# A rank-16 adapter matmul: semaphores set by hand, and the scheduler's context closed behind the first loads

## The chip, the core and the metric

The kernel runs on one core of a Trainium2 chip. The metric is the device time of one execution in microseconds. The kernel before takes 165.16 us, the median of three runs (165.13 to 165.30).

Five engines run their own instruction streams: PE (TensorE: weight loads and matmuls), DVE (VectorE), ACT (ScalarE), POOL (GpSimd) and SP (SyncE, which here only issues DMAs). They meet through semaphores: an instruction may wait until a semaphore has reached a value, and may raise or lower one when it is done. A DMA raises its semaphore by 16 when it has landed, one for each of the 16 DMA engines that share the transfer.

## The reference

```
x_flat = x.reshape(-1, 256)                 # x: 16 x 2048 x 256, so 32768 rows
y = x_flat @ W                              # W: 256 x 256
lora_out = (x_flat @ lora_A) * lora_E       # lora_A: 256 x 16, lora_E: 16
y = y + scale * (lora_out @ lora_B)         # lora_B: 16 x 256, scale 1.0
```

All arrays are float32. The input x and the output have 33.55 MB each.

## The kernel before

The adapter is folded into the weights once: weff = W + lora_A diag(lora_E) lora_B, in bfloat16. PE transposes the two 128-row chunks of lora_A (L92), DVE scales the result by lora_E (ate, L94), PE multiplies it with lora_B (ps_aeb, L104), and DVE adds W (weff, L106). lora_B is first cast to bfloat16 (L89). The identity for the transposes is made on POOL (two instructions in masks.py).

The rows of x are cut into nine blocks of 16, 32 (seven times) and 16 rows for each of 128 partitions: 2 MB or 4 MB. Six buffers ("slots") in SBUF hold a block each. The result is written over the block's input in its slot and stored from there. Loads and stores are all issued by SP, in an order written out by hand: W (L74), loads 0 to 5 (L67), then for each block its store (L71), and behind store 2 the loads 6, 7 and 8, each of which needs the slot of store 0, 1 or 2 and so waits for that store's landing. ACT issues the loads of lora_A, lora_B and lora_E (L76, L78, L80).

A block is worked off in groups of two rows for each partition, 128 groups in all. For a group PE transposes four 128x128 pieces into psum_xt (L114, three buffers), DVE casts them to bfloat16 into xt (L120, four buffers), PE multiplies them with weff into psum_y (L132, three buffers), and ACT copies the result into the slot (L140). PE transposes group n + 1 ahead of the matmuls of group n. The store of a block waits for its last copy.

All of this lies in a tile scheduler's context. The order on each engine is the order of the text (manual_schedule), and the scheduler sets the semaphores: which instruction waits for what, and who raises what. When the context is left (L175) it has each engine drained, lets all engines meet, has POOL clear the semaphores, and lets them meet again. L161 makes the program object, whose start also has all engines meet once.

Of the kernel before, what the change touches and what calls it, by code (L numbers as in the profile page):

```python
# [1 line left out]

# [5 lines left out]

PLAN = [16] + [32] * 7 + [16]

ROWS, SLOTS = 32, 6

LEAD = 6
AFTER = {2: [6, 7, 8]}
CG = 2


@with_exitstack  # L20
def kernel(
    ctx: ExitStack,
    tc: tile.TileContext,
    x: bass.AP,
    W: bass.AP,
    lora_A: bass.AP,
    lora_B: bass.AP,
    lora_E: bass.AP,
    scale: bass.AP,
    out: bass.AP,  # L30
):
    nc = tc.nc
    P = 128
    FP32 = mybir.dt.float32
    BF16 = mybir.dt.bfloat16

    x_flat = x.flatten_outer_dims()
    out_flat = out.flatten_outer_dims()
    N, K = x_flat.shape
    M = out_flat.shape[1]  # L40
    R = lora_B.shape[0]
    KC = K // P
    assert K == M and sum(PLAN) * P == N

    const = ctx.enter_context(tc.tile_pool(name="const", bufs=1))
    slots = ctx.enter_context(tc.tile_pool(name="slots", bufs=SLOTS))
    xTpool = ctx.enter_context(tc.tile_pool(name="xTpool", bufs=4))
    ps_setup = ctx.enter_context(tc.tile_pool(name="ps_setup", bufs=1, space=bass.MemoryType.PSUM))
    ps_xT = ctx.enter_context(tc.tile_pool(name="ps_xT", bufs=3, space=bass.MemoryType.PSUM))
    ps_y = ctx.enter_context(tc.tile_pool(name="ps_y", bufs=3, space=bass.MemoryType.PSUM))  # L50


    ctx.enter_context(tc.manual_schedule())

    starts = [sum(PLAN[:i]) * P for i in range(len(PLAN))]

    def rows_of(flat, i):
        b, r0 = PLAN[i], starts[i]
        return flat[r0:r0 + b * P, :].rearrange("(p b) k -> p b k", b=b)

    held = []

    def load(i):
        t = slots.tile([P, ROWS, K], FP32, name="xy")
        nc.sync.dma_start(out=t[:, :PLAN[i], :], in_=rows_of(x_flat, i))  # L67
        held.append(t)

    def store(i):  # L70
        nc.sync.dma_start(out=rows_of(out_flat, i), in_=held[i][:, :PLAN[i], :])  # L71

    w_sb = const.tile([P, KC, M], FP32)
    nc.sync.dma_start(out=w_sb, in_=W.rearrange("(c p) m -> p c m", p=P))  # L74
    a_sb = const.tile([P, KC, R], FP32)
    nc.scalar.dma_start(out=a_sb, in_=lora_A.rearrange("(c p) r -> p c r", p=P))  # L76
    b_sb = const.tile([R, M], FP32)
    nc.scalar.dma_start(out=b_sb, in_=lora_B)  # L78
    e_sb = const.tile([R, 1], FP32)
    nc.scalar.dma_start(out=e_sb, in_=lora_E[:, None])  # L80

    for i in range(LEAD):
        load(i)

    ident = const.tile([P, P], FP32)
    make_identity(nc, ident)

    b_bf = const.tile([R, M], BF16)
    nc.vector.tensor_copy(out=b_bf, in_=b_sb)  # L89
    ps_at = ps_setup.tile([R, KC, P], FP32, name="ps_at")  # L90
    for c in range(KC):
        nc.tensor.transpose(ps_at[:, c, :], a_sb[:, c, :], ident)  # L92
    ate = const.tile([R, KC, P], BF16)
    nc.vector.tensor_scalar(  # L94
        out=ate,
        in0=ps_at,
        scalar1=e_sb,
        scalar2=float(scale),
        op0=mybir.AluOpType.mult,
        op1=mybir.AluOpType.mult,  # L100
    )
    ps_aeb = ps_setup.tile([P, KC, M], FP32, name="ps_aeb")
    for c in range(KC):
        nc.tensor.matmul(ps_aeb[:, c, :], ate[:, c, :], b_bf, start=True, stop=True)  # L104
    weff = const.tile([P, KC, M], BF16)
    nc.vector.tensor_add(out=weff, in0=w_sb, in1=ps_aeb)  # L106

    groups = [(i, g) for i, b in enumerate(PLAN) for g in range(b // CG)]

    def transposed(i, g):  # L110
        psum_xt = ps_xT.tile([P, CG, KC, P], FP32, name="psum_xt")
        for j in range(CG):
            for c in range(KC):
                nc.tensor.transpose(  # L114
                    psum_xt[:, j, c, :],
                    held[i][:, g * CG + j, c * P:(c + 1) * P],
                    ident,
                )
        xt = xTpool.tile([P, CG, KC, P], BF16, name="xt")
        nc.vector.tensor_copy(out=xt, in_=psum_xt)  # L120
        return xt


    ready = transposed(*groups[0])
    for n, (i, g) in enumerate(groups):
        xt = ready
        if n + 1 < len(groups):
            ready = transposed(*groups[n + 1])
        psum_y = ps_y.tile([P, CG, M], FP32, name="psum_y")
        for j in range(CG):  # L130
            for c in range(KC):
                nc.tensor.matmul(  # L132
                    psum_y[:, j, :],
                    xt[:, j, c, :],
                    weff[:, c, :],
                    start=(c == 0),
                    stop=(c == KC - 1),
                )

        nc.scalar.copy(out=held[i][:, g * CG:(g + 1) * CG, :], in_=psum_y)  # L140
        if (g + 1) * CG == PLAN[i]:
            store(i)
            for later in AFTER.get(i, []):
                load(later)


# [1 line left out]
_INS = ['x', 'W', 'lora_A', 'lora_B', 'lora_E', 'scale']  # L148
_OUTS = [((16, 2048, 256), 'float32')]

_NUMBERS = {'scale': 1.0}


# [26 lines left out]
```

## Time and profile before

| what | us |
|---|---|
| timed runs, median of three | 165.16 |
| span of the profiled execution, first to last instruction | 163.0 |
| what lies around the span (165.16 - 163.0) | 2.16 |
| PE busy in the span | 120.8 |
| DVE, ACT busy | 90.0, 76.3 |
| queue q1 (SP's loads and stores), share of 16 DMA engines | 96.7% |
| bytes moved, mean rate | 67.56 MB, 414 GB/s |

The profiled execution is one execution, taken by the hardware profiler; its own time is its span, and the time around it is known only against the timed runs. Busy shares are averages over the whole span; the page's table of 40 slices (4.1 us each) shows where they lie. The chain of waits follows the last instruction back to what released it. "SPq" is the queue of SP, in which it issues DMAs and waits. A DMA's issue (about 0.45 us on SP or ACT) is not its transfer; the time from issue to landing stands apart.

### The profile page before, as it was taken

The numbers are of one execution on the slowest core, as the hardware profiler recorded it, in microseconds if no ns is written. First come the engines' busy times: TensorE is split into PE (matmuls) and PEld (weight loads), VectorE is DVE, ScalarE is ACT, GpSimd is POOL, SyncE is SP. The second block draws the span as 40 slices with busy tenths as digits, with TensorE's granted clock in tenths as the row PEclk, the third lists the DMA queues.
The fourth block names the chain that finished last, engine by engine and source line by source line (L and its number), as shares of the span: only waits on it lengthen the run. The fifth ranks groups of instructions, "written<-read, shape, count | busy, mean of one in ns | idle before, by whom it ended". The sixth has DMA issues, their size and how long they took to land.

```text
span 163.0 us, 2547 instructions
## 1 busy us (share of the span) xinstructions
PE 120.8 (74%) x1028; PEld 100.9 (62%) x1028; DVE 90.0 (55%) x131; ACT 76.3 (47%) x129; POOL 0.7 (0%) x6
## 2 busy tenths in 40 slices
PE   0189799999999999999999799999999910000000
PEld 0068588888888888888888588888888800000000
DVE  0156477777777777777777667777777700000000
ACT  0036465666666665666666546665666620000000
POOL 1000000000000000000000000000000000000000
PEclk9999999999999999999999999999999995555555
DMA  5999999998998999999999999999999999999992
GB/s 151 428 474 434 394 491 398 410 491 382 420 474 386 392 410 466 418 438 418 450 430 418 442 434 402 432 450 418 422 434 442 422 442 426 442 418 434 434 394 113
DMA packets 3211, 67.56 MB, mean 414 GB/s; under 512 B 624, under 2 KB 896, under 8 KB 896
## 3 DMA queue, kind: packets, MB, share of 16 engines
q1 hardware_dynamic: 2864, 67.37, 96.7%
q8 instruction: 8, 0.13, 0.3%
q10 hardware_dynamic: 336, 0.03, 0.2%
q14 instruction: 3, 0.02, 0.0%
HBM read 33.85 MB, written 33.55 MB: 414 GB/s over the span
## 4 chain that ended last, share of the span: by engine, by line
DMA 55%; PE 23%; ACT 1%; SPq 1%; DVE 0%; issue 0%
DMA xy<-in_x_dram 28%; DMA out_dram<-xy 27%; PE psum_y L132 12%; PE psum_xt L114 11%; ACT xy L140 1%; DVE xt L120 0%; SPq L67 0%; SPq L74 0%
## 5 line engine op out<-in xcount | busy, mean ns | idle before, releaser
L120 DVE CAST xt<-psum_xt 128x512 bf16<-128x512 f32 x128 | 88.6, 692 | 32.5 <-PE psum_xt L114 32.5
L140 ACT COPY xy<-psum_y 128x512 f32<-128x512 f32 x128 | 75.0, 586 | 46.5 <-PE psum_y L132 46.5
L114 PE MATMUL psum_xt<-ident,xy 128*128 128x128 f32 x512 | 77.8, 276 | 2.6 <-DMA xy<-in_x_dram 2.6
L132 PE MATMUL psum_y<-weff,xt 128*128 128x256 bf16 x512 | 78.0, 275 | 0.3 <-DVE xt L120 0.3
L114 PEld LDWEIGHTS psum_xt<-ident,xy 128*128 128x128 f32 x512 | 60.8, 142 | 5.0 <-issue 2.9
L132 PEld LDWEIGHTS <-xt 128*128 128x128 bf16 x512 | 40.0, 98 | 17.0 <-DVE xt L120 0.9
L140 ACT ACT_TABLE_LOAD x1 | 1.3, 1283 | 9.3 <-DMA xy<-in_x_dram 9.3
L92 PE MATMUL ps_at<-ident,a_sb 128*16 128x128 f32 x2 | 0.6, 394 | 4.1 <-DMA a_sb<-in_lora_A_dram 4.1
L89 DVE CAST b_bf<-b_sb 16x256 bf16<-16x256 f32 x1 | 0.3, 281 | 5.8 <-DMA b_sb<-in_lora_B_dram 5.8
L104 PE MATMUL ps_aeb<-b_bf,ate 16*128 16x256 bf16 x2 | 0.6, 402 | 3.8 <-DVE ate L94 3.8
L104 PEld LDWEIGHTS <-ate 16*128 16x128 bf16 x2 | 0.1, 104 | 4.2 <-DVE ate L94 4.2
L92 PEld LDWEIGHTS ps_at<-ident,a_sb 128*16 128x16 f32 x2 | 0.1, 87 | 4.0 <-issue 4.0
L94 DVE TENSOR_SCALAR ate<-ps_at,e_sb 16x256 bf16<-16x256 f32 x1 | 0.5, 471 | 1.8 <-DMA e_sb<-in_lora_E_dram 1.8
L106 DVE TENSOR_TENSOR weff<-w_sb,ps_aeb 128x512 bf16<-128x512 f32 x1 | 0.7, 689 | 0.7 <-PE ps_aeb L104 0.7
masks.py:199 POOL TENSOR_SCALAR_AFFINE_SELECT ident<-ident 128x128 f32<-128x128 f32 x1 | 0.3, 292 | 0.1
masks.py:197 POOL MEMSET ident<- 128x128 f32 x1 | 0.2, 204 | 0.3 <-POOLq L161 0.3
L161 POOL MEMSET const-bfloat16-1.0<- 128x1 bf16 x1 | 0.1, 101 | 0.0
L161 POOL MEMSET const-uint8-127<- 128x1 uint8 x1 | 0.1, 101 | 0.0
L161 POOL MEMSET const-float32-0.0<- 128x1 f32 x1 | 0.1, 98 | 0.2 <-issue 0.2
L161 POOL MEMSET const-float32-1.0<- 128x1 f32 x1 | 0.1, 98 | 0.0
## 6 DMA issues: line engine op xcount, KB each, us to landing
xy<-in_x_dram SPq DMA_DIRECT2D x7, 4096.0 KB, 29.0
out_dram<-xy SPq DMA_DIRECT2D x7, 4096.0 KB, 37.4
xy<-in_x_dram SPq DMA_DIRECT2D x2, 2048.0 KB, 16.1
out_dram<-xy SPq DMA_DIRECT2D x2, 2048.0 KB, 36.9
w_sb<-in_W_dram SPq DMA_DIRECT2D x1, 256.0 KB, 3.0
a_sb<-in_lora_A_dram ACTq DMA_DIRECT2D x1, 16.0 KB, 3.2
b_sb<-in_lora_B_dram ACTq DMA_DIRECT2D x1, 16.0 KB, 4.5
e_sb<-in_lora_E_dram ACTq DMA_DIRECT2D x1, 0.1 KB, 6.0
```

The source lines that it names most:

```text
L89: nc.vector.tensor_copy(out=b_bf, in_=b_sb)
L92: nc.tensor.transpose(ps_at[:, c, :], a_sb[:, c, :], ident)
L94: nc.vector.tensor_scalar(out=ate, in0=ps_at, scalar1=e_sb, scalar2=float(scale), op0=mybir.AluOpType.mult, op1=mybir.AluOpType.mult,)
L104: nc.tensor.matmul(ps_aeb[:, c, :], ate[:, c, :], b_bf, start=True, stop=True)
L106: nc.vector.tensor_add(out=weff, in0=w_sb, in1=ps_aeb)
L114: nc.tensor.transpose(psum_xt[:, j, c, :], held[i][:, g * CG + j, c * P:(c + 1) * P], ident,)
L120: nc.vector.tensor_copy(out=xt, in_=psum_xt)
L132: nc.tensor.matmul(psum_y[:, j, :], xt[:, j, c, :], weff[:, c, :], start=(c == 0), stop=(c == KC - 1),)
L140: nc.scalar.copy(out=held[i][:, g * CG:(g + 1) * CG, :], in_=psum_y)
L161: nc = _bacc.Bacc("TRN2", target_bir_lowering=False, num_devices=1)
```

## The change

The context is closed inside the kernel function, and everything behind it is written without the scheduler.

- Buffers in SBUF and PSUM are taken from the program object directly, in the same number and size.
- Every semaphore is the kernel's own (class Count): one for each small input, for each load and for each store, and six for the steps of the engines.
- W's load and loads 0 to 5 are issued by SP in a block that is marked as critical, the three small loads by ACT in a second such block. Then the context is closed and compiled, so that what it does on leaving (drain, meeting, clearing, meeting) stands there.
- All that follows is the same work in the same order on each engine, with waits written out: two ahead of a group's matmuls (cast done, psum_y free), two ahead of its cast (transposes done, xt free), one ahead of its copy, one ahead of a store, one ahead of loads 6 to 8. PE waits for a load at a block's first group.
- At the end each engine waits for the final values of some semaphores and subtracts them, so that they are zero again: twelve on PE, five on DVE, one on ACT, ten on SP, the last of these for the last store.

The core of the diff (declarations of sizes and the unchanged launch left out):

```diff
+class Count:
+    def __init__(self, nc, name):
+        self.sem = nc.alloc_semaphore(name)
+        self.total = 0
+
+    def by(self, ins, n=1):
+        self.total += n
+        ins.then_inc(self.sem, n)
+        return self.total
...
-    ctx.enter_context(tc.manual_schedule())
...
     def load(i):
-        t = slots.tile([P, ROWS, K], FP32, name="xy")
-        nc.sync.dma_start(out=t[:, :PLAN[i], :], in_=rows_of(x_flat, i))
-        held.append(t)
+        s_ld[i].by(nc.sync.dma_start(out=slot(i), in_=rows_of(x_flat, i)), 16)
 
     def store(i):
-        nc.sync.dma_start(out=rows_of(out_flat, i), in_=held[i][:, :PLAN[i], :])
+        s_st[i].by(nc.sync.dma_start(out=rows_of(out_flat, i), in_=slot(i)), 16)
+
+    def spent(engine, count):
+        engine.wait_ge(count.sem, count.total).then_inc(count.sem, -count.total)
...
+    with tc.tile_critical(no_gpsimd_drain=True):
+        s_w.by(nc.sync.dma_start(out=w_sb, in_=W.rearrange("(c p) m -> p c m", p=P)), 16)
+        for i in range(LEAD):
+            load(i)
+    with tc.tile_critical(no_gpsimd_drain=True):
+        s_a.by(nc.scalar.dma_start(out=a_sb, in_=lora_A.rearrange("(c p) r -> p c r", p=P)), 16)
+        s_b.by(nc.scalar.dma_start(out=b_sb, in_=lora_B), 16)
+        s_e.by(nc.scalar.dma_start(out=e_sb, in_=lora_E[:, None]), 16)
+    tc.close()
+    tc.compile()
+
+    s_id.by(nc.gpsimd.memset(ident, 0.0))
+    nc.gpsimd.wait_ge(s_id.sem, 1)
+    s_id.by(nc.gpsimd.affine_select(
+        out=ident, in_=ident, compare_op=mybir.AluOpType.not_equal, fill=1.0, base=0,
+        pattern=[[-1, P]], channel_multiplier=1))
...
+    nc.vector.wait_ge(s_b.sem, 16)
+    s_v.by(nc.vector.tensor_copy(out=b_bf, in_=b_sb))
+    nc.tensor.wait_ge(s_a.sem, 16)
+    nc.tensor.wait_ge(s_id.sem, 2)
     for c in range(KC):
-        nc.tensor.transpose(ps_at[:, c, :], a_sb[:, c, :], ident)
+        at_done = nc.tensor.transpose(ps_at[:, c, :], a_sb[:, c, :], ident)
+    s_set.by(at_done)
+    nc.vector.wait_ge(s_e.sem, 16)
+    nc.vector.wait_ge(s_set.sem, 1)
...
-    def transposed(i, g):
-        psum_xt = ps_xT.tile([P, CG, KC, P], FP32, name="psum_xt")
+    def transposed(n):
+        i, g = groups[n]
+        if g == 0:
+            nc.tensor.wait_ge(s_ld[i].sem, 16)
         for j in range(CG):
             for c in range(KC):
...
+        s_t.by(done)
+        nc.vector.wait_ge(s_t.sem, n + 1)
+        if n >= 4:
+            nc.vector.wait_ge(s_m.sem, n - 3)
+        s_v.by(nc.vector.tensor_copy(out=xt[n % 4], in_=ps_xt[n % 3]))
...
+        nc.tensor.wait_ge(s_v.sem, ready0 + n + 1)
+        if n >= 3:
+            nc.tensor.wait_ge(s_y.sem, n - 2)
         for j in range(CG):
             for c in range(KC):
...
+        s_m.by(done)
+        nc.scalar.wait_ge(s_m.sem, n + 1)
+        s_y.by(nc.scalar.copy(out=slot(i)[:, g * CG:(g + 1) * CG, :], in_=ps_y[n % 3]))
         if (g + 1) * CG == PLAN[i]:
+            nc.sync.wait_ge(s_y.sem, n + 1)
             store(i)
             for later in AFTER.get(i, []):
+                nc.sync.wait_ge(s_st[later - SLOTS].sem, 16)
                 load(later)
+
+    for count in [s_a, s_id, s_v] + s_ld:
+        spent(nc.tensor, count)
+    for count in [s_b, s_e, s_w, s_set, s_t]:
+        spent(nc.vector, count)
+    spent(nc.scalar, s_m)
+    for count in [s_y] + s_st:
+        spent(nc.sync, count)
```

## The prediction

> **What bounds the kernel now.** I read the page's slices and queues first, then the chain, then SP's waits, then the timeline of the first 12 us, and last the rows of line 175.
>
> ```profile
> PE   0189799999999999999999799999999910000000
> ...
> DMA  5999999998998999999999999999999999999992
> ...
> q1 hardware_dynamic: 2864, 67.37, 96.7%
> ...
> DMA 55%; PE 23%; ACT 1%; SPq 1%; DVE 0%; issue 0%
> ```
>
> The DMA engines are full from the second slice to the last but one. Queue q1 (SP's loads and stores) fills 96.7% of 16 engines. PE ends in slice 33 of 40. So the span is: the time to the first packet, 67.37 MB at the rate of the engines, and what follows the last packet. Compute matters only if a store is issued so late that the queue runs empty.
>
> ```profile
> SPq L71 <- ACT xy L140: 85.7, 8, 14.3
> SPq L67 <- DMA out_dram<-xy: 32.7, 3, 14.1
> SPq L175 <- DMA out_dram<-xy: 29.5, 3, 15.1
> ```
>
> SP waits for compute before eight stores, and after the last one only for landings: compute is ahead of the queue. How far, the single records say. Stores 2, 7 and 8 are issued at 50.10, 124.78 and 132.12. The last packets of the transfers ahead of them (stores 1, 6 and 7) end at 73.9, 147.0 and 156.7. The first q1 packet (2.04) comes 1.3 us after its issue (0.74). So store 7 may be 147.0 - 1.3 - 124.8 = 20.9 us later before the slowest DMA engine is empty, store 2 22.5 us, store 8 23.3 us. Store 7 has the least cover.
>
> ```profile
> 0.73 0.50 ACTq L76 DMA_DIRECT2D a_sb<-in_lora_A_dram  x1
> 0.74 0.44 SPq L74 DMA_DIRECT2D w_sb<-in_W_dram  x1
> 1.23 3.53 SPq L67 DMA_DIRECT2D xy<-in_x_dram  x6
> 1.25 0.49 ACTq L78 DMA_DIRECT2D b_sb<-in_lora_B_dram  x1
> 1.77 0.44 ACTq L80 DMA_DIRECT2D e_sb<-in_lora_E_dram  x1
> ...
> 7.87 0.47 DVE L94 TENSOR_SCALAR ate<-ps_at,e_sb 16x256 bf16<-16x256 f32 x1 [1.83 <-DMA e_sb<-in_lora_E_dram]
> ...
> 11.16 1.03 PE L132 MATMUL psum_y<-weff,xt 128*128 128x256 bf16 x4
> ```
>
> All inputs are issued by 4.8 us, ACT's three beside SP's. The first real matmul (11.16) hangs on lora_E, although that is 64 bytes: it lands 6.0 us after its issue, behind A and B in q10.
>
> ```profile
> L175 POOLq EVENT_SEMAPHORE  x4: 17/17/17, 162.3 to 162.9; - x4
> L175 SPq DRAIN  x2: 7/7/7, 162.3 to 162.6; - x2
> ...
> L175 POOLq EVENT_SEMAPHORE_RANGE_CLEAR  x1: 96/96/96, 162.6 to 162.6; - x1
> ```
>
> That is line 175 after 162.3: two rounds of all engines with a semaphore clear between, until 163.0. The last q1 packet ends at 161.57, and SP's wait for it passes at 162.06.
>
> **The change part by part.** The profiled execution has a span of 163.0; the median of the timed runs is 165.16, so 2.16 us lie around the span, which I leave as they are.
>
> *Closing barriers gone from the end.* From SP's pass (162.06) to the end are 0.94 us: two more waits 0.06 apart, drains, two rounds. What comes instead are SP's ten waits that subtract; nine pass while earlier stores land, the tenth takes 0.03 to 0.06. Gain 0.88 to 0.91, on the path: -0.9.
>
> *Barriers at the front.* SP reaches them after its seven issues: 0.74 + 7 x 0.49 = 4.2. Two rounds took 0.64 at the end (162.31 to 162.95), so the other engines are free at about 4.9 (7 if ACT's block comes after). Cover: load 0 lands at 9.2 and lora_E at 7.8 or later. The identity's two POOL instructions (0.20 and 0.29) then end by 5.7, A's transposes (0.58) by 6.3: nothing. Entry into the first marked block: at least one semaphore step, 0.04 by the first barrier's rows (POOL 0.611, SP 0.653), at most a whole barrier (0.67, the span's first). I take 0.1, nearest to a step.
>
> *SP's load 4 no longer waits for lora_A's landing* (3.12 to 3.94): nothing, five transfers are queued ahead.
>
> *ACT's three loads in a second marked block.* The diff does not say whether block two may start before block one is over. Both ends: side by side, ACT issues at 0.73 as now; one after the other, ACT waits until SP has issued seven transfers, 4.2, plus a drain and two or three semaphore steps, 4.45. I take the later: the scheduler treats a marked block as one unit, ended by a drain of its engines, and keeps such units in order. Then what do A, B and E cost behind the bulk? Lower bound: the rows of now, 3.2, 4.5 and 6.0 us from issue to landing, so E at 5.5 + 6.0 = 11.5, 4 later than now. Upper bound, by the packet records: on one DMA engine A's 64-byte pieces start 49 ns apart as long as W's 1 KB pieces (46 ns) lie between, and 7 ns apart once W is through: one piece of each queue in turn. A has 256 pieces, 16 for each engine, and a completion. In the new order a turn is a piece of x: 0.61 us (16 KB, load 0) until 8.5, then 1.21 (32 KB). First piece 4.45 + 1.8 (A's 0.73 to 2.51) = 6.2; four turns to 8.5; thirteen more x 1.21 = 15.7: 24.2. B and E follow: now 3.5 us from A's end to E's, at 0.61 a turn 5.5 turns, then 6.7 us: 30.9, visible 0.4 later at 31.3 instead of 7.8. I take this end, since it is the same queue in the same trace.
>
> The Trainium skill ("DMA: Bandwidth & Descriptors", section on queues, rings and completion order) says an engine takes its queue rows in turn but drains a whole packet of some 9 to 17 descriptors each time. By that A would need one or two turns, and E would land near 12. The 49 ns do not agree with it.
>
> So the first matmul moves by 23.5 us. Two waits of compute for loads that are then long there fall away: 1.2 ahead of block 1 (PE's longest wait for a load) and 1.3 ahead of block 6 (store 5 at 95.45 against 50.10 + 3 x 14.67 = 94.11). Store 7 is 23.5 - 2.5 = 21.0 late, against a cover of 20.9: used up, 0.1 over. Store 2 is 22.3 late, against 22.5.
>
> *ACT's table load* (1.28 from 9.28, now while ACT waits) may come behind the first hand-written wait. Three psum_y buffers, 2.75 of PE's work, cover it.
>
> *Waits written by hand.* Each of 128 groups has two waits before its matmuls and two before its cast. Now the cast itself waits for PE, and weight load and matmul each carry one wait. By hand, the instruction behind can take one, and the other may stand ahead of it. A wait that stands ahead costs 0.075 before the instruction starts (ate's: 7.795, then 7.870; PE's: 3.953, then 4.029). PE and DVE wait for each other: from a group's transposes (41.09) over its cast (41.72) to its matmuls (42.47) are 1.38, PE has 1.31 of work meanwhile (three fours of 0.44), and two groups take 1.83 (casts at 39.89 and 41.72). A delay d in that loop costs d/2 a group. So 0 (both waits carried as now) to 0.075 a group (one ahead on each engine). I take the middle, 0.0375; there is no nearer row. To store 7 are 120 groups: 4.5 us (0 to 9). Alone it is hidden by the 20.9; behind the late weights it is not.
>
> A page has a price for this: "VectorE: DVE Perf Modes" in the Trainium skill, in its section on the drain that can't be avoided, found that a semaphore after each copy costs nothing extra. By that the sum would lose its 4.5; the 0.075 of the two rows speaks against.
>
> Sum for the likeliest case: 165.16 - 0.9 + 0.1 + 0.1 + 4.5 = **169.0 us**. In span, 166.8.
>
> **The rivals.**
> 1. *ACT's block runs beside SP's.* A, B and E are issued at 0.73 as now, E lands at 7.8, the waits cost at most 9 of 20.9: all hidden. 165.16 - 0.9 + 0.1 = 164.4: faster. For it: different engines, nothing shared in the trace's first microseconds. Against: the order of marked blocks.
> 2. *Late weights, free waits.* Blocks in order, but PE and DVE carry their waits as now. Store 7 is 0.1 over its cover, within the error of the 31.3: 164.4 to 165.0. It decides at a shift of 20.9 at store 7.
> 3. *A's pieces go through in one turn.* E near 12, shift of store 7 about 4 + 9 at most: hidden, 164.4. The Trainium skill's rule on packets above is this one; the 49 ns are against it.
> 4. *The first load is later.* If the entry into a block costs a whole barrier, 0.67, first packet at 2.7 and the gain is nearly gone: 165.16 - 0.9 + 0.7 = 165.0, no change.
>
> **How the numbers follow.** A measurement of this kernel tells some 0.2% from no change (164.83 to 165.49). Forecast case 0.56, of which 0.02 within 0.2%; rival 1 0.22; rival 2 0.11, of which 0.02 within; rival 3 0.05; rival 4 0.06, of which 0.04 within, 0.01 on each side. Faster 0.22 + 0.09 + 0.05 + 0.01 = 0.37; same 0.08; slower 0.54 + 0.01 = 0.55. The likeliest case alone goes from 165.7 (waits at 0.01 a group) to 173.5 (waits at 0.075: 9.0 in place of 4.5). Since faster cases hold more than 2 in 10, the range begins at theirs, 164.2.
>
> **What would show it.** Right: ACT's issue of lora_A at 4 to 5 us, ate at about 31, first matmul of line 132's successor near 34.5, casts 0.95 or more apart, store 7 issued after 146, and a hole in the DMA row at 75 to 80 or 147 to 152. Nothing of barriers after the last landing, and the span ending within 0.1 us of SP's last wait. Wrong: ACT's issues before 2 us, or ate before 15: then DMA stays full and the time is 164.4. A first q1 packet later than 2.5 would be rival 4. A compute rate of 0.917 a group with late weights is rival 2.

## The result and the profile after

The changed kernel takes **167.38 us** (median of four runs, 166.94 to 167.82), the kernel before 165.16 (median of four as well). The ratio is 1.0136, with a 95% interval of 1.0122 to 1.0150: slower. The profiled execution is the longest of the four, 167.82, with a span of 166.5 and 1.32 around it.

Rows of the page of the kernel after: busy tenths in 40 slices of 4.16 us, bytes moved in each, the chain that ended last, and the landing times of two of ACT's loads (the last number of the last two lines, us from issue to landing):

```profile
PE   0000001199999999999999999999999999999000
...
DMA  5999999999999999959899989999999999999994
GB/s 161 409 485 394 466 418 414 457 394 480 401 421 457 346 449 447 419 228 394 374 378 425 453 386 496 374 362 457 425 392 464 401 449 421 441 429 449 417 390 209
...
PE 72%; DMA 16%; DVE 1%; ACTq 1%; ACT 0%; issue 0%
...
a_sb<-in_lora_A_dram ACTq DMA_DIRECT2D x1, 16.0 KB, 23.5
...
e_sb<-in_lora_E_dram ACTq DMA_DIRECT2D x1, 0.1 KB, 26.3
```

PE starts its main work in the ninth slice instead of the third. The DMA row has one hole, in the 18th slice (70.8 to 74.9 us), where the rate falls to 228 GB/s. The chain that ended last was mostly DMA and is now 72% PE: it runs from lora_E's landing through PE to the stores. A chain of this kind says which work was late, not that PE is too slow: PE's busy time has hardly changed (121.5 us against 120.8).

The start of the span and the issue of store 2, from the timeline of the kernel after (start, length, engine, line, operation; in brackets the idle time ahead of it and what ended it):

```profile
0.94 0.44 SPq L84 DMA_DIRECT2D w_sb<-in_W_dram  x1
1.43 2.99 SPq L74 DMA_DIRECT2D xy<-in_x_dram  x6
5.03 0.43 ACTq L88 DMA_DIRECT2D a_sb<-in_lora_A_dram  x1
5.49 0.49 ACTq L89 DMA_DIRECT2D b_sb<-in_lora_B_dram  x1
6.00 0.44 ACTq L90 DMA_DIRECT2D e_sb<-in_lora_E_dram  x1
7.41 0.20 POOL L94 MEMSET ident<- 128x128 f32 x1 [6.97 <-POOLq L92]
...
32.31 0.47 DVE L110 TENSOR_SCALAR ate<-ps_at,e_sb 16x256 bf16<-16x256 f32 x1 [2.17 <-DMA e_sb<-in_lora_E_dram]
...
35.27 1.03 PE L148 MATMUL psum_y<-weff,xt 128*128 128x256 bf16 x4
...
73.97 0.33 SPq L77 DMA_DIRECT2D out_dram<-xy  x1
```

ACT's first issue stands at 5.03, 0.6 behind the end of SP's seventh; before, it was at 0.73. lora_E is there at 32.3 instead of 7.8, and the first real matmul starts at 35.27 instead of 11.16, 24.1 us later. Store 2 is issued at 73.97 instead of 50.10 (23.9 late), store 7 at 147.31 instead of 124.78 (22.5 late).

SP's waits in the kernel after (us in total, times, longest):

```profile
SPq L77 <- ACT xy L153: 131.3, 9, 37.3
SPq L74 <- DMA out_dram<-xy: 11.5, 2, 11.3
SPq L80 <- SPq L80: 11.0, 2, 6.1
```

SP now waits for ACT's last copy before all nine stores, 131.3 us in all. The waits for landings that stood ahead of loads 6 to 8 have shrunk from three (14.1 at the longest) to two.

Where the time went can be read from the end of each transfer, as a mean over the 16 DMA engines, taken from the packet records. A piece is one packet of a load or store: 32 KB of a block of 32 rows, 16 KB of a block of 16. From the end of one transfer to the end of the next the two kernels agree within 0.16 us, but for two steps. From store 1 to store 2 it is 12.96 us instead of 9.72 (+3.2): each engine stands idle for 2.3 us on average, which is the hole, and slow pieces of store 2 make the other 0.9. From load 7 to load 8 it is 5.85 instead of 4.92 (+0.9), where 37 of load 8's 128 pieces of 16 KB take more than 0.65 us, up to 1.37, instead of 0.61. The last store ends at 164.63 instead of 160.21 on the mean engine (+4.4), and on the slowest at 166.13 instead of 161.57. Behind that the span goes on for 0.37 us, before for 1.43. So the two profiled executions differ by 4.56 - 1.06 = 3.5 us in the span, 166.5 against 163.0, and by 0.5 the other way around it (1.3 against 1.8, as measured for the kernel before in the experiments' executions).

### The profile page after: what moved, and what is told of

It is laid out like the page before. It is cut to its first block, busy times and chain, and to the rows that moved or that the text cites. A ratio compares the mean times of both kernels' runs of the same rounds, so it can differ in the third digit from the quotient of the medians.

```text
span 166.5 us, 2676 instructions
## 1 busy us (share of the span) xinstructions
PE 121.5 (73%) x1028; PEld 101.9 (61%) x1028; DVE 90.0 (54%) x131; ACT 76.4 (46%) x129; POOL 0.7 (0%) x6
## 4 chain that ended last, share of the span: by engine, by line
PE 72%; DMA 16%; DVE 1%; ACTq 1%; ACT 0%; issue 0%
PE psum_y L148 37%; PE psum_xt L129 35%; DMA e_sb<-in_lora_E_dram 16%; DVE xt L137 0%; PE ps_aeb L115 0%; ACT xy L153 0%; ACTq L89 0%; DVE ate L110 0%; ACTq L88 0%; ACTq L92 0%; ACTq L87 0%
## 5 line engine op out<-in xcount | busy, mean ns | idle before, releaser
L153 ACT COPY xy<-psum_y 128x512 f32<-128x512 f32 x128 | 75.1, 587 | 70.8 <-PE psum_y L148 70.8
L148 PEld LDWEIGHTS psum_y<-weff,xt 128*128 128x128 bf16 x512 | 40.3, 98 | 17.1 <-DVE xt L137 0.9
## 6 DMA issues: line engine op xcount, KB each, us to landing
a_sb<-in_lora_A_dram ACTq DMA_DIRECT2D x1, 16.0 KB, 23.5
```

The costliest lines, as they stand in the source:

```text
L148: done = nc.tensor.matmul(ps_y[n % 3][:, j, :], xt[n % 4][:, j, c, :], weff[:, c, :], start=(c == 0), stop=(c == KC - 1))
L153: s_y.by(nc.scalar.copy(out=slot(i)[:, g * CG:(g + 1) * CG, :], in_=ps_y[n % 3]))
```

## The experiments

The kernel before took 164.97 and 164.98 us on the two chips used here; ratios are against it. "One block" is the second kernel below, and most others are read against it.

**1. ACT's loads in the same marked block as SP's.** This undoes the order of the two blocks and keeps all else.

```diff
             load(i)
-    with tc.tile_critical(no_gpsimd_drain=True):
         s_a.by(nc.scalar.dma_start(out=a_sb, ...), 16)
```

> The changed kernel with ACT's three small loads in the same marked block as SP's loads, so that neither engine waits for the other. Theory (late weights are the whole loss: E lands at 32.3 instead of 7.8 because the second block starts when the first is over): ACT issues A at about 1, E lands near 8, the first group's matmul is near 11.5, store 2 near 50.5, no hole in the DMA row; time 165.16 - 0.9 = 164.3 (164.0 to 164.6). Rival (the hand-written semaphores or the closing at the front cost the transfers something by themselves): 166.5 or more, with the hole or slower transfers still there.

Measured: **163.95 us** (163.88 to 164.34), ratio 0.9941 (0.9929 to 0.9954): faster than both kernels, and just under the expected range. Its page and its timeline:

```profile
DMA  5999999999899989999999999999999999999994
...
a_sb<-in_lora_A_dram ACTq DMA_DIRECT2D x1, 16.0 KB, 3.0
...
e_sb<-in_lora_E_dram ACTq DMA_DIRECT2D x1, 0.1 KB, 6.1
```

```profile
0.91 0.49 ACTq L87 DMA_DIRECT2D a_sb<-in_lora_A_dram  x1
0.95 0.42 SPq L84 DMA_DIRECT2D w_sb<-in_W_dram  x1
```

ACT and SP issue side by side, lora_A lands 3.0 us after its issue instead of 23.5, store 2 is issued at 50.35, and the DMA row has no hole. So the whole loss hangs on the second block: 167.38 - 163.95 = 3.4 us. Without it the change gains 1.0.

**2. The three small loads on SP, behind load 0.** One block, one queue, no ACT: if A's pieces are slow because they take turns with another queue's, they should not be slow inside SP's own.

```diff
-        for i in range(LEAD):
+        load(0)
+        s_a.by(nc.sync.dma_start(out=a_sb, ...), 16)   # then B and E, on nc.sync too
+        for i in range(1, LEAD):
             load(i)
-    with tc.tile_critical(no_gpsimd_drain=True):
...
```

> The changed kernel with one marked block, all of it on SP: W, load 0, then A, B and E, then loads 1 to 5. A, B and E now stand in the same queue as the bulk, behind load 0, so no turns with another queue. Theory: they land just behind load 0's last pieces, near 9.5 to 10; first group's matmul near 13; store 2 near 52; no hole; 164.3 (164.0 to 164.6). Rival (a small load beside the bulk is slow whatever its queue): E lands at 20 or later and the time is 164.3 to 167, by the cover of 22.5 at store 2.

Measured: 164.19 us (163.86 to 165.5), ratio 0.9953 (0.9937 to 0.9968). lora_A lands 7.6 us after its issue at 1.93, behind W and load 0 (which ends at 8.3 to 8.9), and lora_E at 9.9. Bytes in front cost the time of those bytes; the 23.5 us come only where the small pieces stand in a queue of their own beside the large ones.

**3. The kernel before, with lora_A issued late.** ACT copies a piece of W into A's buffer first, so its three loads wait for W's landing. No hand-written semaphore, no moved barrier.

```diff
     a_sb = const.tile([P, KC, R], FP32)
+    nc.scalar.copy(out=a_sb[:, 0, :], in_=w_sb[:, 0, :R])
     nc.scalar.dma_start(out=a_sb, in_=lora_A.rearrange("(c p) r -> p c r", p=P))
```

> The kernel before, scheduler and closing barriers as they were, but ACT first copies a few elements of W into A's buffer, so that the loads of A, B and E are issued when W has landed, some 4 us later. The output is the reference's, since A's load overwrites them. Theory: a delay of 4 us in the issue alone makes A take 17 turns with pieces of x: E lands at 29 to 33, store 2 is 21 to 25 us late, the DMA engines run empty ahead of store 2, and the time is 165.2 to 169.5, most likely 168. Rival (the loss in the changed kernel is of its semaphores or its front): E lands by 12 and the time stays at 165.2.

Measured: 166.79 us (166.66 to 166.97), ratio 1.0106 (1.0092 to 1.0121). From its timeline and its page (busy tenths of the DMA engines, and lora_E's landing):

```profile
3.68 0.42 ACTq L77 DMA_DIRECT2D a_sb<-in_lora_A_dram  x1
```

```profile
DMA  5999999999999899999989999999999999999991
...
e_sb<-in_lora_E_dram ACTq DMA_DIRECT2D x1, 0.1 KB, 24.4
```

Three microseconds of delay at the issue become 21.3 at the landing (29.1 against 7.8), under the old scheduler as well. Store 2 is 20.6 late, and 1.8 us are lost, half of the 3.4 us above. But the DMA row has no hole here: by the packet records every engine goes from store 1 to store 2 without a gap (0.02 us idle on average). The loss lies in slow pieces, 0.6 us at store 2 and 1.2 at load 8. So a store that comes as late as this costs time even when the queue does not run empty, and the expectation, which put the loss down to empty engines, was right in its range and wrong in its reason.

**4. Half of lora_A.** The changed kernel, with only the first 128 rows of lora_A loaded and used for both halves.

```diff
-        s_a.by(nc.scalar.dma_start(out=a_sb, in_=lora_A.rearrange("(c p) r -> p c r", p=P)), 16)
+        s_a.by(nc.scalar.dma_start(out=a_sb[:, 0, :], in_=lora_A[:P, :]), 16)
...
-        at_done = nc.tensor.transpose(ps_at[:, c, :], a_sb[:, c, :], ident)
+        at_done = nc.tensor.transpose(ps_at[:, c, :], a_sb[:, 0, :], ident)
```

> The changed kernel, loading only the first 128 rows of A (128 pieces of 64 bytes, 8 for each DMA engine, in place of 256 and 16) and using them for both halves, so that the output is not the reference's. The order of the blocks stays. Theory (one piece of each queue in turn, 1.21 us a turn): A lands 8 x 1.21 = 9.7 us earlier, E at 32.3 - 9.7 = 22.6, store 2 14 us late against a cover of 22.5: no hole, 164.3 (164.0 to 164.7). Rival by the Trainium skill's rule in DMA: Bandwidth & Descriptors (a whole packet of 9 to 17 descriptors in a turn): A's landing hardly changes, and the time stays at 167.4.

Measured: 164.65 us (164.53 to 165.48), ratio 0.9982 (0.9968 to 0.9996). From its page:

```profile
DMA  5999999998999999999999999999999999999992
...
a_sb<-in_lora_A_dram ACTq DMA_DIRECT2D x1, 8.0 KB, 13.8
...
e_sb<-in_lora_E_dram ACTq DMA_DIRECT2D x1, 0.1 KB, 17.7
```

8 KB less, which 400 GB/s move in 0.02 us, bring lora_E 8.6 us earlier (23.7 against 32.3) and save 2.7 us. Store 2 is issued at 64.66, 14.6 late, and there is no hole. Store 2 and load 8 take no longer than in the kernel before (9.74 and 4.87 us). Blocks in order cost little, then, if what lands late has few pieces: 0.7 over one block, with the last store on the mean DMA engine no later (160.41 against 160.60) and on the slowest 0.8 later.

**5. lora_A twice.** The changed kernel loads it once more, into a buffer that nobody reads, ahead of the real one.

```diff
     with tc.tile_critical(no_gpsimd_drain=True):
+        s_a2.by(nc.scalar.dma_start(out=a2_sb, in_=lora_A.rearrange("(c p) r -> p c r", p=P)), 16)
         s_a.by(nc.scalar.dma_start(out=a_sb, ...), 16)
```

> The changed kernel, with A loaded once more, ahead of the load that is used, into a buffer of its own: 17 more turns for each DMA engine in ACT's queue. Theory (one piece of each queue in turn; beyond the cover a delay is paid in full): E lands 17 x 1.21 = 20.6 later, at 52.9, or somewhat earlier when the bulk's first store is reached, since then nothing is queued beside it; store 2 is 20 us later than in the changed kernel, which pays for all of it: 167.4 + 19 to 21 = 187 (184 to 189). Rival by the Trainium skill's rule in DMA: Bandwidth & Descriptors (a packet of 9 to 17 descriptors in a turn): one or two turns more, 167.4 to 170.

Measured: 186.47 us (185.19 to 187.54), ratio 1.1296 (1.1257 to 1.1335). From its page:

```profile
DMA  5999999999992180099089999999999999999995
...
e_sb<-in_lora_E_dram ACTq DMA_DIRECT2D x1, 0.1 KB, 44.2
```

16 KB of pieces that nobody reads cost 19.1 us. lora_E lands at 50.7, and now stores 0, 1 and 2 all come too late: the steps to their ends are 6.9, 9.9 and 5.5 us longer than before. Over experiments 4 and 5 a piece of lora_A for each DMA engine is worth 8.6 / 8 = 1.08 and 18.4 / 17 = 1.08 us (sixteen pieces and a completion in the second). The packet records of the changed kernel show the turn itself: on one engine A's 64-byte pieces start at 9.454, 10.671, 11.887 and 13.104, that is 1.217 apart, with one 32 KB piece of x between two of them. Where one load of x ends and the next begins, the end of the load, a packet of 4 bytes, is a turn too, so that two of A's pieces follow each other within 13 ns. With one such short turn among eight the mean is the 1.08.

The Trainium skill ("DMA: Bandwidth & Descriptors", section on queues, rings and completion order) has an engine drain a whole packet of some 9 to 17 descriptors from a queue before it turns to the next. That would put A through in one or two turns; the 1.217 us between single pieces do not agree with it, unless a packet here holds a single descriptor.

**6. Store 2 late, compute early.** One block; SP waits for 26 more groups before store 2, so that it is issued when the changed kernel's was. Loads 6 to 8 stand behind it in SP's order, so load 6 is issued late as well, at 74.36 instead of 64.75 in one block; its transfer stands behind store 2's in any case.

```diff
-            nc.sync.wait_ge(s_y.sem, n + 1)
+            nc.sync.wait_ge(s_y.sem, n + 27 if i == 2 else n + 1)
```

> The kernel with one marked block (163.95), but SP waits before store 2 for the copy of a group 26 groups later than block 2's last one, so that store 2 is issued 26 x 0.917 = 23.8 us later, as in the changed kernel; weights and compute stay early. Theory (the loss is the queue running empty ahead of store 2, and nothing else of the late compute): the same loss as the changed kernel against this one, 3.4: 167.4 (166.6 to 167.8), with a hole of 3 us ahead of store 2 and slower pieces at load 8. Rival (late compute loses something itself, by PE's work being spread to the end): the loss is 2 or less, 166 or below.

Measured: 167.79 us (167.68 to 168.05), ratio 1.0170 (1.0157 to 1.0183), 3.8 over one block. From its page:

```profile
PE   0189999999999999999999269999999960000000
...
DMA  4999999989999999969899989999999999999985
```

PE begins its main work in the third slice, as in the kernel before, and yet the DMA row has the changed kernel's hole in the 18th slice. Store 2 is issued at 73.98. The step to its end is 12.38 us (+2.7 over before, of which the engines are idle for 1.9) and the one to load 8's 5.90 (+1.0). So a late store 2, with the loads behind it, is enough for the loss. Late compute is not needed for it, nor is a late store 7.

**7. The two blocks swapped.** ACT's block first, SP's second.

> The changed kernel with the two marked blocks in the other order: ACT's three loads first, then SP's. Theory (a block starts when the one before is over): SP's issue of W moves from 0.95 to 0.95 + 3 x 0.5 + 0.25 = 2.7, so the first packet of the bulk comes 1.7 us later; A, B and E have the DMA engines to themselves and land by 5; no hole later; 163.95 + 1.7 = 165.7 (165.2 to 166.0). Rival (blocks overlap where their engines differ, and ACT's delay in the changed kernel has another reason): 164.0.

Measured: 166.11 us (165.94 to 166.32), ratio 1.0062 (1.0048 to 1.0077). From its timeline:

```profile
0.97 0.43 ACTq L84 DMA_DIRECT2D a_sb<-in_lora_A_dram  x1
...
2.98 0.44 SPq L88 DMA_DIRECT2D w_sb<-in_W_dram  x1
```

Now SP waits for ACT's block: W is issued at 2.98 instead of 0.95, and the time is 2.2 over one block, about the 2.0 by which the bulk starts later (expected was a start 1.7 later, so the time lies 0.1 above its range). lora_E lands at 3.6. The two blocks run in the order of the text whichever engine they are on.

**8. Two meetings of all engines put back at the end.** One block, and behind the last subtracting wait:

```diff
     for count in [s_y] + s_st:
         spent(nc.sync, count)
+    nc.all_engine_barrier()
+    nc.all_engine_barrier()
```

> The kernel with one marked block (163.95), with two meetings of all engines put behind SP's last wait, where the scheduler's closing had them. It prices the closing by itself. Theory: two rounds cost 0.3 to 0.45 each in the span (0.94 from SP's pass to the end before, 0.07 in the kernel with one block), so 163.95 + 0.7 = 164.65, and if the time around the span (1.8 before, 1.3 in the kernel with one block) also belongs to all engines ending together, 0.5 more: 165.1. Rival (what lies around the span has nothing to do with the barriers): time less span stays at 1.3, 164.6.

Measured: 165.04 us (164.84 to 165.9), ratio 1.0008 (0.9997 to 1.0020): the gain is gone. 165.04 - 163.95 = 1.09 us. The end of the second meeting, in the group of line 169 (engine, operation, count: shortest, median and longest in ns, first and last start in us), and the last instruction of the kernel after, in the group of its line 80:

```profile
L169 PEldq EVENT_SEMAPHORE  x1: 51/51/51, 163.0 to 163.0; - x1
```

```profile
L80 SPq EVENT_SEMAPHORE  x1: 17/17/17, 166.5 to 166.5; - x1
```

SP's last wait passes at 162.39 and the span ends at 163.0, so 0.6 of the 1.1 lie in the span. The other 0.5 lie around it: 1.84 us in this profiled execution, against 1.31 in that of one block, and 1.8 to 1.9 in all of its twelve runs against 1.3 to 1.4 in the five of one block.

## Why the forecast of slower was right, and why its sum was not

The direction and most of the chain came out as forecast: the blocks run in order, lora_A takes turns piece by piece with the bulk, the weights are late by some 24 us, and the DMA engines run empty at a store. The time lies 1.6 below the forecast. But two terms of the sum were wrong by some 4 us each, in opposite directions, so that the number came out close by luck. The direction owes something to luck too: without the 4.5 us of the waits, which did not exist, the same sum gives 164.5, faster. In truth it was the case of rival 2 (late weights, free waits), with a price of its own that the prediction had missed.

**Closing barriers gone, -0.9.** In the span this is right: 0.37 us follow the last packet instead of 1.43, and SP's last wait, at 166.49, is the end. But I had left what lies around the span as it was, and it falls from 1.8 to 1.3. The term was too small by 0.5, and experiment 8 shows this half and the other: two meetings cost 0.6 in the span and 0.5 around it. The 2.16 of the prediction set the median of the timed runs against the span of another execution. One block gains 1.0 and not the 1.4 of the two parts, because its last packet ends 0.5 later on the slowest engine (162.07 against 161.57; load 0 ends 0.3 later on the mean engine already); why, no run here shows.

**Barriers at the front, nothing.** Right. The other engines are free at 7.41, forecast 7 for ACT's block behind SP's, and all that waits for them has to wait for lora_A anyway.

**Entry into the marked block, +0.1.** W is issued 0.2 later, at 0.94, but the first packet of its queue starts at 2.03, before at 2.04: nothing. Rival 4 fell by this.

**Blocks in order.** Right, and shown by experiments 1 and 7. ACT's issue was forecast at 4.45 and came at 5.03, since a drain, three semaphore steps and a branch lie between (4.47 to 5.03). Experiment 1 makes rival 1 happen; its 164.4 came out at 163.95.

**A, B and E behind the bulk.** Forecast at 31.3, it is 32.3, of which 0.6 are the later issue. Rival 3 fell with the 1.217 us between pieces.

**Late weights, +0.1.** This step failed. It measured +3.2 at store 2 (2.3 of idle engines, 0.9 of slow pieces) and +0.9 at load 8 (slow pieces). The shift and the cover account for the idle engines; for slow pieces the prediction had no term:

- The shifts were larger than forecast: store 2 23.9 late instead of 22.3, store 7 22.5 instead of 21.0. Of the 2.5 us of waits that were to fall away ahead of store 7 only 1.6 did.
- The cover was read at the slowest DMA engine: store 1's last packet in the kernel before ends at 73.9 there, but at 71.6 on the fastest and 72.5 on the mean one. Each engine that runs empty loses its share. The 1.3 us from issue to first packet, taken from W at the start, were too long as well: in the changed kernel store 2 is issued at 73.97 and its first pieces start at 74.80 to 74.95, 0.9 later. With the mean and the 0.9 the cover of store 2 is 72.5 - 0.9 - 50.1 = 21.5, not 22.5; its shift of 23.9 is 2.4 over. From the mean end of store 1 (72.5) to the first pieces of store 2 (74.9 on the mean engine) the trace shows just that, and slow pieces of store 2 (15 of them, from 82 to 84 us, take over 1.29 us instead of 1.21) make up the rest of the 3.2.
- Store 7's cover is 145.7 - 0.9 - 124.8 = 20.0 by the same measure, less than its shift, and still decided nothing. The hole at store 2 had by then moved every later transfer by more than 4 us, so its cover was larger by as much. The first hole pays for the later ones. I had searched for the least cover over all stores, and named the wrong one.

Even with the prediction's own shift, this cover would have given 22.3 - 21.5 = 0.8 us at store 2, to which the prediction gave no cost.

**Hand-written waits, +4.5.** This step failed too: they cost nothing. A stretch of the timeline of the kernel after, when it is in step:

```profile
130.63 0.69 DVE L137 CAST xt<-psum_xt 128x512 bf16<-128x512 f32 x1 [0.18 <-PE psum_xt L129]
...
131.59 0.69 DVE L137 CAST xt<-psum_xt 128x512 bf16<-128x512 f32 x1 [0.27 <-PE psum_xt L129]
...
132.47 0.69 DVE L137 CAST xt<-psum_xt 128x512 bf16<-128x512 f32 x1 [0.18 <-PE psum_xt L129]
```

And the waits that stand alone, ahead of PE's matmuls in the kernel after and, below, ahead of DVE's casts in the kernel before:

```profile
L145 PEldq EVENT_SEMAPHORE  x125: 51/51/51, 38.0 to 152.5; - x125
```

```profile
L120 DVEq EVENT_SEMAPHORE  x124: 21/21/21, 13.7 to 129.2; - x124
```

Two groups take 132.47 - 130.63 = 1.84 us, before 1.83; stores 3 and 4 are issued at 88.64 and 103.31, 14.67 apart as before. The forecast said 0.95 or more between casts. Of a pair of waits, the one that comes last is carried by the weight load, or by the cast itself, as in the kernel before. The other one stands as an instruction of its own (PE has 141 of them instead of 12, of 51 ns), but it is satisfied long before and passes beside running matmuls. The 0.075 of the prediction were taken from rows where the wait that stood ahead was also the last to be satisfied. The middle of 0 and 0.075 was a guess about which of the two stands ahead. For PE the trace of before could not tell. For DVE it could: 124 waits stood alone ahead of the casts there already, at 0.917 us a group, and the changed kernel has as many.

The Trainium skill ("VectorE: DVE Perf Modes", section on the drain that can't be avoided) says that a semaphore after each copy costs nothing extra. No run here has casts without one: they raise a semaphore in both kernels. What the 0.917 us a group of both kernels show is that the waits standing alone cost nothing here.

Put together: 165.16 - 1.0 (all of the change but the order of the blocks, by experiment 1) + 3.4 (that order) = 167.6, measured 167.38. This checks nothing by itself, since both terms come from the same 163.95; the 0.2 left over is the kernel before on two chips (165.16 and 164.97). What stands apart is the price in the trace, +4.4 us at the end of the last store on the mean engine, and experiment 6, which brings the loss back by a late store 2.

**Still open: the slow pieces.** In the four runs whose store 2 is issued 20 us late or more (the changed kernel and experiments 3, 5 and 6), slow pieces at store 2 cost 0.6 to 1.0 us on each engine and load 8 takes 0.9 to 1.2 longer; in the other runs neither is seen. Experiment 6 shows that a late store 2 with early compute is enough for them, and experiment 3 that no empty queue is needed. In these four the engines' ends of load 7 lie within 1.7 us of each other; in the others they lie 2.2 us or more apart. Behind load 8 the queue turns from loads to stores, so engines that turn at the same moment might get in each other's way. Two things in the traces speak against it. In the changed kernel load 8's slow pieces start from 107.2 to 110.3 us, and the first piece of store 3 only at 110.3. And at the other turn, from load 5 to store 0, the step is 10.2 us in both kernels, although the ends of load 4 lie 1.8 us apart in the kernel before and 0.8 in the one after. Why the pieces are slow, no run here shows.

## What to carry to other kernels

Read how many pieces a load has, and what lies in the other queues while it runs: 256 pieces of 64 bytes beside 32 KB pieces took 23.5 us instead of 3.2, and every DMA engine paid nearly one large piece for each small one. Issue such loads ahead of the bulk or inside its queue, and look in the trace whether what is written side by side also starts side by side. When you ask how late an issue may come, take the mean over the DMA engines and not the last one, and begin with the earliest place where the queue can run empty, since a hole there moves all later ones out of reach. Leave some margin besides: in experiment 3 the store came just in time, and 1.8 us were lost.

## What was not expected of the hardware

- The time around the span depends on how the kernel ends: 1.3 us when the engines end one by one, each after its own last wait, and 1.8 to 1.9 when all of them meet at the end (experiment 8).
- A turn between two queues is one piece of each at any size seen here: 64 bytes against 1 KB (49 ns between A's pieces, in the kernel before) and 64 bytes against 32 KB (1.217 us). The 4-byte end of a transfer is a turn as well.
- With a store issued 20 us late or more, pieces slow down where no engine waits: 37 of load 8's 128 pieces of 16 KB take more than 0.65 us instead of 0.61, worth 0.9 us on each engine, and some of store 2's pieces of 32 KB take over 1.29 instead of 1.21. The cause is open.
